# A seventh and a fourth pair by seven products in the two halves of the output projection, and a fixed order of the tail's passage to its seeded banks

## The chip, the cores and the metric

The kernel runs on one core of one Trainium2 chip. The metric is the device time of one execution in microseconds (us), of which smaller is better. Three runs of the kernel before gave 905.26 us in the median (904.65 to 905.49).

## The reference, cut to what matters

One layer of a hybrid decoder (DEPTH is 1, so the recurrence layer never runs), in float32, for one sequence of 256 tokens, width 2048 and branch width 4096:

```
h = rmsnorm(x, norm_g); h, gate = adaln(h, c, ada_w, ada_b)
b_gate, c_gate, v, g = split(h @ w_in, 4)              # 256 x 2048 by 2048 x 16384
y = b_gate * causal_conv(c_gate * v, conv_w) * silu(g) # 256 x 4096
x = x + gate * (y @ w_out)                             # 256 x 4096 by 4096 x 2048
return rmsnorm(x, final_g)
```

The change touches the last product, `y @ w_out`, and what leads from it to the output.

## The kernel before, in words

**Split products.** Every float32 operand of a matmul is split into a high part (a cast on ScalarE, `split_hi`, L352) and a low part (a subtraction on VectorE, `split_lo`, L357), and a product is three matmuls: high by high, high by low, low by high (`triple`, L722). Each weight tile of 128 x 2048 elements (1 MB) is loaded by SyncE's queue (`load_o`, L711), cast by ScalarE, subtracted by VectorE, and used by TensorE.

**Rings.** Weight tiles live in three rings of three buffers: `lo` holds the raw weights of the output projection and the sums made of them, `hi` the high parts, `raw` the low parts. A load can be issued only when the last reader of the buffer's former content is through, which is nearly always a VectorE subtraction; a cast and a subtraction wait in the same way for TensorE to be through with the buffers that they overwrite.

**The output projection.** The 4096 rows of `w_out` are 32 blocks of 128, taken in 16 pairs; `y` of a pair is one tile of 128 x 2 x 2 x 256 (two blocks, high and low, 256 tokens). `columns` (L771) takes 1024 output columns at a time and walks the pairs in an order written by hand. A plain pair costs one split and 24 matmuls of 512 columns (2 token tiles, 2 blocks, 2 column halves, 3 each). A pair in `sevens` goes by a Strassen form instead (`seven`, L736): seven products, 21 matmuls, of four sums of the weights (L742, L744, L745 on VectorE) and four sums of `y` (`token_forms`, L632), with two casts and two subtractions (L743 and L746 for the weights, L352 and L357 for their sums). The sums of `y` of the pairs in `SEVEN` are made while the projection in runs, where each pair's `y` arises. Three products go to separate banks (`p1`, `p6`, and `p75` with two) that `gather` (L761) adds up on VectorE and ScalarE behind the last such pair, through a 128 x 512 scratch `u2` at the end of the tile `big`.

- First 1024 columns: the pairs in the order 0, 1, 10, 2, 11, 3, 12, 4, 13, 5, 14, 6, 15, 7, 8, 9, those from 10 on by seven. Behind it VectorE adds the banks to the gathered sums (L809) and `gated` (L726) multiplies by the gate and adds the residual, in the time of the second 1024 columns.
- Second 1024 columns: 0, 1, 2, 10, 3, 13, 11, 4, 14, 12, 5, 15, with 10, 11, 12 by seven. Pairs 6 to 9 (`LAST`) come after it: first for column half 2 (`halves[0]`, both token tiles), then for column half 3, whose weights are multiplied by the gate first (L862). For half 3, what is there so far is gated, added to the residual and written back by ScalarE into two banks `po[0]` and `po[1]`, one for each token tile (L847 to L850: the seeded banks); the last 48 matmuls add to them, the first 24 to `po[0]`, the last 24 to `po[1]`.
- `finish(t)` (L815) squares `po[t]` on ScalarE with its sum (L877), takes the root (L818, with a change of ScalarE's function table before the first), the reciprocal (L819), and scales and stores four pieces of 128 x 512 (L820 to L829).

**What sets the order.** The order on each engine is that of a scheduler which lays the traced instructions out by its own times; `later`, `behind` and `in_order` (L165 to L194) bend it by hand. Each engine runs its list in order.

**Token tiles.** The normalised tokens lie in `hT` (14 of the 16 blocks of 128) and `hT2` (the last two); the buffers are used again, that of `hT` for `big` (residual, `final_g`, `u2`), that of `hT2` for the sums of `y` of pair 15.

Of the kernel before, what the change touches and what calls it, by code (L numbers as in the profile page):

```python
# [8 lines left out]
F32 = mybir.dt.float32  # L9
# [108 lines left out]
def short_conv_layer(ctx: ExitStack, tc: tile.TileContext, x, c, norm_g, ada_w, ada_b, w_in, conv_w, w_out, final_g, out):  # L118
# [175 lines left out]
    KB = KT - 2  # L294
    hT = hpool.tile([P, KB, 2 * T], F32R, tag="big", name="hT")
    hT2 = hpool.tile([P, KT - KB, 2 * T], F32R, tag="big2", name="hT2")

    def tokens(k, part):
        return (hT[:, k] if k < KB else hT2[:, k - KB])[:, part * T : (part + 1) * T]
# [329 lines left out]
    SEVEN = range(10, 16)  # L629
    forms = {}  # L630

    def token_forms(pair, u):  # L632

        sums = zs[0][:, 1].rearrange("p a (b f) -> p (a b) f", f=P)
        a11, a12 = u[:, 0, 0:P], u[:, 1, 0:P]
        a21, a22 = u[:, 0, P:T], u[:, 1, P:T]
        s1n, s2, s3, s4 = (sums[:, j] for j in range(4))
        nc.vector.scalar_tensor_tensor(out=s1n, in0=a21, scalar=-1.0, in1=a22, op0=ALU.mult, op1=ALU.subtract)
# [3 lines left out]
        if pair < 14:  # L642
            form = adap.tile([P, ASLOT], F32R, tag="at", name="form", bufs=4).rearrange("p (h s f) -> p h s f", h=2, f=P)
            hi, lo = form[:, 0], form[:, 1]
        elif pair == 14:
            hi, lo = (adap.tile([P, 512], F32R, tag="gv", name="form_g").rearrange("p (s f) -> p s f", f=P) for _ in range(2))
        else:
            form = hpool.tile([P, 2, 4, P], F32R, tag="big2", name="form_h")
            hi, lo = form[:, 0], form[:, 1]
        forms[pair] = hi, lo  # L650
        nc.scalar.copy(hi, sums)
        nc.vector.tensor_tensor(out=lo, in0=sums, in1=hi.bitcast(F32), op=ALU.subtract)

    for ct in range(NS, NCT, 2):
        for q in QUARTERS:
# [28 lines left out]
            else:  # L684
                nc.vector.tensor_tensor(out=u, in0=bank, in1=u, op=ALU.mult)
                split_y(ys[ct // 2], u)
                if ct // 2 in SEVEN:
                    token_forms(ct // 2, u)
# [5 lines left out]
    big = hpool.tile([P, 3 * D + W], F32, tag="big", name="big")  # L694
    xr = big[:, 0 : TT * D].rearrange("p (t f) -> p t f", t=TT)
    fg = big[:, TT * D : 3 * D]
    u2 = big[:, 3 * D :]
# [100 lines left out]
    def wide_bank(name):  # L798
# [5 lines left out]
        0, (0, 1, 10, 2, 11, 3, 12, 4, 13, 5, 14, 6, 15, 7, 8, 9), SEVEN,  # L804
# [10 lines left out]
    def finish(t):  # L815
# [20 lines left out]
        2 * W, (0, 1, 2, 10, 3, 13, 11, 4, 14, 12, 5, 15), SEVEN[0:3],  # L836
# [8 lines left out]
    for t in range(TT):  # L845
        c = ends[t][:, 1]
        nc.vector.tensor_tensor(out=c, in0=halves[1][:, t], in1=c, op=ALU.add)  # L847
        nc.vector.tensor_tensor(out=c, in0=c, in1=gate(3), op=ALU.mult)
        nc.vector.tensor_tensor(out=c, in0=c, in1=xr[:, t, 3 * W : 4 * W], op=ALU.add)
        nc.scalar.copy(po[t], c)  # L850
# [6 lines left out]
    late = []  # L857
    for ep in LAST:
# [4 lines left out]
        hi, lo = split(raw, SLOT, "raw")  # L863
# [39 lines left out]
```

## Time and profile before

| | |
|---|---|
| runs | 905.26 us median, 904.65 to 905.49 |
| profiled execution, its own time | 905.34 us |
| its span in the trace | 903.6 us |
| PE busy, DVE busy, ACT busy | 888.2, 670.2, 482.4 us |
| mean granted clock of PE | 0.998 |

The page gives for each engine its busy time, for each line of the kernel the number and mean length of its instructions and what the engine had waited for, and the chain of work that ended last. PE is TensorE, PEld its weight loads, DVE VectorE, ACT ScalarE, SPq the DMA queue of SyncE. In a timeline a row is one instruction or a run of equal ones: start, length, engine, line, operation, output and inputs, count, and in brackets the idle time of the engine just before it with what ended it.

### The profile page before, as it was taken

The numbers are of one execution on the slowest core, as the hardware profiler recorded it, in microseconds if no ns is written. First come the engines' busy times: TensorE is split into PE (matmuls) and PEld (weight loads), VectorE is DVE, ScalarE is ACT, GpSimd is POOL, SyncE is SP. The second block draws the span as 40 slices with busy tenths as digits, with TensorE's granted clock in tenths as the row PEclk, the third lists the DMA queues.
The fourth block names the chain that finished last, engine by engine and source line by source line (L and its number), as shares of the span: only waits on it lengthen the run. The fifth ranks groups of instructions, "written<-read, shape, count | busy, mean of one in ns | idle before, by whom it ended". The sixth has DMA issues, their size and how long they took to land.

```text
span 903.6 us, 16403 instructions
## 1 busy us (share of the span) xinstructions
PE 888.2 (98%) x7000; PEld 851.0 (94%) x7000; DVE 670.2 (74%) x661; ACT 482.4 (53%) x427; POOL 87.3 (10%) x95
## 2 busy tenths in 40 slices
PE   7999999999999999999999999999999999999996
PEld 4899999999999999999999999999999988888884
DVE  5889989888888867765875677565555578889685
ACT  6767866665548756644433434443434435544443
POOL 0000000000000132024324303320000000000000
PEclk9999999999999999999999999999999999999999
DMA  9999999999998587687988888866666486675652
GB/s 309 366 368 368 363 313 354 353 369 351 351 328 286 162 279 247 187 257 236 287 238 241 257 279 263 248 211 200 188 187 190 138 304 209 212 251 163 214 182 94
DMA packets 159594, 235.01 MB, mean 260 GB/s; under 512 B 6804, under 2 KB 105284, under 8 KB 159136
## 3 DMA queue, kind: packets, MB, share of 16 engines
q1 hardware_dynamic: 156384, 226.56, 76.7%
q0 software_dynamic: 3008, 7.34, 2.8%
q8 instruction: 55, 0.90, 0.4%
q14 instruction: 19, 0.16, 0.1%
q10 hardware_dynamic: 128, 0.04, 0.0%
HBM read 224.49 MB, written 2.10 MB: 251 GB/s over the span
## 4 chain that ended last, share of the span: by engine, by line
PE 90%; DMA 4%; DVE 2%; ACT 1%; SPq 1%; issue 1%; ACTq 0%
PE mm_b L491 39%; PE mm_s L491 36%; PE mm_w L722 7%; PE mm_o L722 5%; PE mm L722 4%; DMA at<-in_ada_w_dram 2%; DVE lo L357 1%; SPq L231 1%; DMA raw_s<-in_sc_w_in_dram 1%; ACT hi L352 1%; DMA x<-in_x_dram 1%; DMA raw_o<-in_sc_w_out_dram 1%; PE tp_g L481 0%; DVE raw_o L862 0%; ACT mm_s L524 0%
## 5 line engine op out<-in xcount | busy, mean ns | idle before, releaser
L491 PE MATMUL mm_s<-hT,hi 128*128 128x256 f32 x2048 | 350.3, 277 | 1.8 <-ACT hT L328 1.0
L491 PE MATMUL mm_b<-hT,hi 128*128 128x256 f32 x2048 | 348.2, 276 | 0.0
L491 PEld LDWEIGHTS mm_s<-hT,hi 128*128 128x128 f32 x2048 | 308.1, 188 | 2.4 <-ACT hT L328 1.2
L491 PEld LDWEIGHTS mm_b<-hT,hi 128*128 128x128 f32 x2048 | 308.6, 188 | 0.0
L491 PE MATMUL mm_b<-hT,lo 128*128 128x256 f32 x1024 | 282.6, 276 | 0.0
L491 PE MATMUL mm_s<-hT,lo 128*128 128x256 f32 x1024 | 282.0, 277 | 0.1
L357 DVE TENSOR_TENSOR lo<-raw,hi 128x2048 fp32r<-128x2048 f32 (+1 forms) x66 | 151.8, 2301 | 101.4 <-ACT hi L352 101.1
L352 ACT CAST hi<-raw 128x2048 fp32r<-128x2048 f32 (+1 forms) x66 | 123.7, 1875 | 191.6 <-PE mm_b L491 150.7
L491 PEld LDWEIGHTS mm_b<-hT,lo 128*128 128x128 f32 x1024 | 192.2, 188 | 0.0
L491 PEld LDWEIGHTS mm_s<-hT,lo 128*128 128x128 f32 x1024 | 191.7, 188 | 0.3 <-DVE lo L357 0.3
L357 DVE TENSOR_TENSOR lo<-raw_s,hi 128x2048 fp32r<-128x2048 f32 (+1 forms) x80 | 149.3, 1872 | 39.6 <-ACT hi L352 39.1
L352 ACT CAST hi<-raw_s 128x2048 fp32r<-128x2048 f32 (+1 forms) x80 | 123.9, 1557 | 56.1 <-PE mm_s L491 51.7
L474 DVE SCALAR_TENSOR_TENSOR gv<-at,silu_c,gv 128x512 f32<-128x512 f32 x105 | 78.6, 749 | 3.6 <-DMA at<-in_ada_w_dram 1.9
L512 ACT COPY acc<-mm_s 128x1024 f32<-128x1024 f32 x54 | 54.7, 1013 | 42.4 <-PE mm_s L491 42.3
L357 DVE TENSOR_TENSOR lo<-raw_o,hi 128x2048 fp32r<-128x2048 f32 x23 | 52.5, 2289 | 25.7 <-ACT hi L352 25.7
L352 ACT CAST hi<-raw_o 128x2048 fp32r<-128x2048 f32 x23 | 43.8, 1908 | 48.4 <-PE mm_o L722 17.3
L722 PE MATMUL mm_o<-hi,y 128*128 128x512 f32 x188 | 59.0, 389 | 0.0
L722 PE MATMUL mm_w<-hi,y 128*128 128x512 f32 x184 | 58.8, 389 | 0.0
L623 POOL TENSOR_TENSOR gacc<-gacc,z 128x512 f32<-128x512 f32 x28 | 45.9, 1639 | 119.3 <-DMA z<-gacc 119.3
L617 DVE SCALAR_TENSOR_TENSOR gacc<-at_g,silu_c,gacc 128x512 f32<-128x512 f32 x60 | 45.9, 764 | 8.0 <-DMA at_g<-in_ada_w_dram 6.9
L621 POOL DMA_DIRECT2D z<-gacc x28 | 15.7, 561 | 330.6 <-DVE acc L558 284.9
L722 PEld LDWEIGHTS mm_o<-hi,y 128*128 128x128 f32 x188 | 35.3, 188 | 7.3
(152 smaller groups left out, 675.4 us busy)
## 6 DMA issues: line engine op xcount, KB each, us to landing
raw<-in_sc_w_in_dram SPq DMA_DIRECT2D x64, 1024.0 KB, 5.8
raw_s<-in_sc_w_in_dram SPq DMA_DIRECT2D x47, 1024.0 KB, 7.7
raw_o<-in_sc_w_out_dram SPq DMA_DIRECT2D x32, 1024.0 KB, 5.2
at<-in_ada_w_dram SPq DMA_DIRECT2D x114, 256.0 KB, 7.8
raw_s<-in_sc_w_in_dram SPq DMA_DIRECT2D x33, 512.0 KB, 6.7
at_g<-in_ada_w_dram SPq DMA_DIRECT2D x32, 512.0 KB, 7.8
at<-in_ada_w_dram SPq DMA_DIRECT2D x6, 512.0 KB, 9.3
x<-in_x_dram SPq DMA_DIRECT2D x4, 512.0 KB, 6.2
```

The costliest lines, as they stand in the source:

```text
L231: nc.sync.dma_start(at[:, :, s, :], adas[:, j : j + kk, s, 0 : NK0 * P])
L352: nc.scalar.copy(hi[:, :n], raw[:, :n])
L357: nc.vector.tensor_tensor(out=lo[:, :n], in0=raw[:, :n], in1=hi[:, :n].bitcast(F32), op=ALU.subtract)
L474: nc.vector.scalar_tensor_tensor(out=gv, in0=at4[:, i], scalar=c_k, in1=gv, op0=ALU.mult, op1=ALU.add)
L491: mm = last_mm[0] = nc.tensor.matmul(dst, w, h[k], start=begins and left, stop=ends, skip_group_check=True)
L512: nc.scalar.copy(acc[ch, q], bank)
L617: nc.vector.scalar_tensor_tensor(out=ga, in0=at3[:, i, :], scalar=s, in1=ga, op0=ALU.mult, op1=ALU.add)
L621: nc.gpsimd.dma_start(turned[0 : P - away], ga[away:P])
L623: nc.gpsimd.tensor_tensor(out=ga, in0=ga, in1=turned, op=ALU.add)
L722: nc.tensor.matmul(dst, y[a], b, start=opens and i == 0, stop=ends and i == 2, skip_group_check=True)
```

## The change

1. The token tiles are cut 12, 2, 2 (`hT`, `hT2`, `hT3`), and `big` loses `u2`, so that a second buffer of the size of `hT2` comes free for sums of `y`. `gather` uses a half of `ends[1]` as its scratch.
2. Pair 9 joins `SEVEN`. Its sums of `y` are made late: `late_form` adds the high and low part of `y` of pair 9 again and calls `token_forms`, in the first 1024 columns behind the load of the seventh pair of the order.
3. First 1024 columns: 0, 1, 10, 2, 11, 3, 12, 4, 13, 5, 14, 6, 15, 9, 7, 8, with seven pairs by seven (10 to 15 and 9).
4. Second 1024 columns: 0, 1, 2, 10, 3, 11, 4, 12, 5, 13, 14, 15, with four pairs by seven (10 to 13).
5. The passage to the seeded banks is split by token tile and put in a fixed order on each engine with the two gated weight tiles of half 3: gate the first weights, `move(0)`, split them, gate the second, cast them, `move(1)`, subtract. The matmuls into `po[0]` are traced behind both splits, those into `po[1]` still behind `finish(0)`; the scheduler orders them anew. What follows on half 2 is held behind that order.

```diff
-    KB = KT - 2
+    KB = KT - 4
     hT = hpool.tile([P, KB, 2 * T], F32R, tag="big", name="hT")
-    hT2 = hpool.tile([P, KT - KB, 2 * T], F32R, tag="big2", name="hT2")
+    hT2 = [hpool.tile([P, 2, 2 * T], F32R, tag=f"big{i}", name=f"hT{i}") for i in (2, 3)]
...
-    SEVEN = range(10, 16)
+    SEVEN = range(9, 16)
+    LAST_FORM = 9
...
-            form = hpool.tile([P, 2, 4, P], F32R, tag="big2", name="form_h")
+            form = hpool.tile([P, 2, 4, P], F32R, tag="big2" if pair == 15 else "big3", name="form_h")
...
-    big = hpool.tile([P, 3 * D + W], F32, tag="big", name="big")
+    big = hpool.tile([P, 3 * D], F32, tag="big", name="big")
...
-        add(u2, p6, ends[0][:, 1])
-        add(ends[1][:, 1], p75[:, 0], u2)
-        add(ends[0][:, 0], p75[:, 1], u2)
+        add(ends[1][:, 0], p6, ends[0][:, 1])
+        add(ends[1][:, 1], p75[:, 0], ends[1][:, 0])
+        add(ends[0][:, 0], p75[:, 1], ends[1][:, 0])
         add(ends[1][:, 0], p75[:, 1], ends[1][:, 1])
+
+    def late_form():
+        u = zs[1][:, 1]
+        y = ys[LAST_FORM]
+        nc.vector.tensor_tensor(out=u, in0=y[:, :, 0].bitcast(F32), in1=y[:, :, 1].bitcast(F32), op=ALU.add)
+        token_forms(LAST_FORM, u)
...
             if loads:
                 loads(n - 4)
+                if n == 6:
+                    late_form()
...
-        0, (0, 1, 10, 2, 11, 3, 12, 4, 13, 5, 14, 6, 15, 7, 8, 9), SEVEN,
+        0, (0, 1, 10, 2, 11, 3, 12, 4, 13, 5, 14, 6, 15, 9, 7, 8), (10, 11, 12, 13, 14, 15, 9),
...
-        2 * W, (0, 1, 2, 10, 3, 13, 11, 4, 14, 12, 5, 15), SEVEN[0:3],
+        2 * W, (0, 1, 2, 10, 3, 11, 4, 12, 5, 13, 14, 15), (10, 11, 12, 13),
...
+    def move(t):
+        c = ends[t][:, 1]
+        nc.vector.tensor_tensor(out=c, in0=halves[1][:, t], in1=c, op=ALU.add)
+        nc.vector.tensor_tensor(out=c, in0=c, in1=gate(3), op=ALU.mult)
+        nc.vector.tensor_tensor(out=c, in0=c, in1=xr[:, t, 3 * W : 4 * W], op=ALU.add)
+        nc.scalar.copy(po[t], c)
...
+    with in_order():
+        raw_a = gated_piece(LAST[0])
+        move(0)
+        late = [(LAST[0], *split(raw_a, SLOT, "raw"))]
+        raw_b = gated_piece(LAST[1])
+        hi_b = split_hi(raw_b, SLOT)
+        move(1)
+        late.append((LAST[1], *split_lo(raw_b, SLOT, hi_b, "raw")))
+    for ep, hi, lo in late:
         out_mm(po[0], 0, ep, hi, lo)
-        late.append((ep, hi, lo))
     for t in range(TT):
         c = ends[t][:, 0]
-        nc.vector.tensor_tensor(out=c, in0=halves[0][:, t], in1=c, op=ALU.add)
-        gated(t, 2 * W, W, c, c, 1)
+        with behind(ended):
+            nc.vector.tensor_tensor(out=c, in0=halves[0][:, t], in1=c, op=ALU.add)
+            gated(t, 2 * W, W, c, c, 1)
```

Up to the output projection every engine's list is as before. Three places of the lists matter for the prediction. The first is VectorE at the end of the first 1024 columns. Before, it stood so, from pair 15's weights and their sums (`raw_o_8725`, `sums_o_8727`) to the plain pair 7 (`raw_o_8765`):

```order
L742 TENSOR_TENSOR sums_o_8727<-raw_o_8725 128x1024
L744 TENSOR_TENSOR sums_o_8727<-raw_o_8725,sums_o_8727 128x512
L745 TENSOR_TENSOR sums_o_8727<-raw_o_8725,sums_o_8727 128x512
L746 TENSOR_TENSOR lo_8729<-raw_o_8725,hi_8728 128x1536
L357 TENSOR_TENSOR lo_8737<-sums_o_8727,hi_8735 128x2048
L357 TENSOR_TENSOR lo_8769<-raw_o_8765,hi_8767 128x2048
```

In the changed kernel pair 15 (`raw_o_8734`, `sums_o_8736`) is followed by pair 9 by seven (`raw_o_8769`, `sums_o_8771`) and then by pair 7 (`raw_o_8809`):

```order
L746 TENSOR_TENSOR lo_8738<-raw_o_8734,hi_8737 128x1536
L742 TENSOR_TENSOR sums_o_8771<-raw_o_8769 128x1024
L357 TENSOR_TENSOR lo_8746<-sums_o_8736,hi_8744 128x2048
L744 TENSOR_TENSOR sums_o_8771<-raw_o_8769,sums_o_8771 128x512
L745 TENSOR_TENSOR sums_o_8771<-raw_o_8769,sums_o_8771 128x512
L746 TENSOR_TENSOR lo_8773<-raw_o_8769,hi_8772 128x1536
L357 TENSOR_TENSOR lo_8781<-sums_o_8771,hi_8779 128x2048
L357 TENSOR_TENSOR lo_8813<-raw_o_8809,hi_8811 128x2048
```

Two pairs by seven now follow each other without a plain one between them, and the first sum of pair 9's weights stands ahead of the last subtraction of pair 15. In these rings the buffer of `raw_o_8769` is that of pair 6's weights, and the buffer of `raw_o_8809` is that of `sums_o_8736`.

The second place is VectorE in the second 1024 columns, ahead of the plain pair 4 (`raw_o_9074`), in the changed kernel; pair 11 is `raw_o_9039`, pair 12 `raw_o_9104`:

```order
L357 TENSOR_TENSOR lo_9013<-raw_o_9009,hi_9011 128x2048
L744 TENSOR_TENSOR sums_o_9041<-raw_o_9039,sums_o_9041 128x512
L745 TENSOR_TENSOR sums_o_9041<-raw_o_9039,sums_o_9041 128x512
L746 TENSOR_TENSOR lo_9043<-raw_o_9039,hi_9042 128x1536
L357 TENSOR_TENSOR lo_9051<-sums_o_9041,hi_9049 128x2048
L742 TENSOR_TENSOR sums_o_9106<-raw_o_9104 128x1024
L357 TENSOR_TENSOR lo_9078<-raw_o_9074,hi_9076 128x2048
```

Before, two plain pairs (3 and 13, then 4 and 14) stood between the pairs by seven, and each sum came behind them; now there is one, and the first sum of pair 12 stands ahead of pair 4's subtraction.

The third place is the end of TensorE's list. Before, the last matmuls into `po[0]` (`mm_1_8868`) and the first into `po[1]` (`mm_1_8869`), 24 matmuls from the end:

```order
L722 MATMUL mm_1_8868<-hi_9340,y9_4461 128x512 x2
L722 MATMUL mm_1_8868<-lo_9342,y9_4461 128x512
L722 MATMUL mm_1_8868<-hi_9340,y9_4461 128x512
L722 MATMUL mm_1_8869<-hi_9321,y6_4444 128x512
L722 MATMUL mm_1_8869<-lo_9323,y6_4444 128x512
```

In the changed kernel, from the last matmuls into `po[0]` (`mm_1_8882`) to the last of all:

```order
L722 MATMUL mm_1_8882<-lo_9349,y9_4462 128x512
L722 MATMUL mm_1_8882<-hi_9343,y9_4462 128x512
L722 MATMUL mm_1_8883<-lo_9349,y8_4461 128x512
L722 MATMUL mm_1_8883<-hi_9343,y8_4461 128x512 x2
L722 MATMUL mm_1_8883<-lo_9349,y8_4461 128x512
L722 MATMUL mm_1_8883<-hi_9343,y8_4461 128x512
L722 MATMUL mm_1_8883<-hi_9343,y9_4462 128x512
L722 MATMUL mm_1_8883<-lo_9349,y9_4462 128x512
L722 MATMUL mm_1_8883<-hi_9343,y9_4462 128x512 x2
L722 MATMUL mm_1_8883<-lo_9349,y9_4462 128x512
L722 MATMUL mm_1_8883<-hi_9343,y9_4462 128x512
```

`po[0]` is now complete 11 matmuls before the end instead of 24: 13 of `po[1]`'s matmuls, those with the first weights of half 3, stand ahead of `po[0]`'s last 11.

More of the change, by code (lines that the diff above doesn't have):

```diff
@@ L290, in short_conv_layer @@
     nc.vector.reciprocal(rstd, rstd)
[L294 removed]
+    KB = KT - 4
     hT = hpool.tile([P, KB, 2 * T], F32R, tag="big", name="hT")
[L296 removed]
+    hT2 = [hpool.tile([P, 2, 2 * T], F32R, tag=f"big{i}", name=f"hT{i}") for i in (2, 3)]
     def tokens(k, part):
[L299 removed]
+        return (hT[:, k] if k < KB else hT2[(k - KB) // 2][:, k % 2])[:, part * T : (part + 1) * T]
     hh_ = [tokens(k, 0) for k in range(KT)]
@@ L641, in token_forms @@
         nc.vector.tensor_tensor(out=s4, in0=a12, in1=s2, op=ALU.subtract)
-        if pair < 14:
+        if 9 < pair < 14:
             form = adap.tile([P, ASLOT], F32R, tag="at", name="form", bufs=4).rearrange("p (h s f) -> p h s f", h=2, f=P)
@@ L686, in short_conv_layer @@
                 split_y(ys[ct // 2], u)
-                if ct // 2 in SEVEN:
+                if ct // 2 in SEVEN and ct // 2 != LAST_FORM:
                     token_forms(ct // 2, u)
@@ L843, in out_mm @@
             triple(bank, y_parts(ep * EP + i, t), hi[:, o], lo[:, o], False, ep == LAST[-1] and i == EP - 1)
[L845 to L850, printed above, removed]
     for ep in LAST:
@@ L856, in short_conv_layer, with gated_piece @@
             out_mm(halves[0][:, t], t, ep, hi, lo)
-    late = []
-    for ep in LAST:
+    def move(t):
[4 more added lines that the diff above has]
+        nc.scalar.copy(po[t], c)
+    def gated_piece(ep):
         raw = w_tile("lo", "raw_o")
```

5 lines of the change are left out of this document (2 added, 3 removed).

## The prediction

> **What bounds the kernel now.** I read the shares, the chain that ended last, and what PE waited for in the output projection (engine, line, what it waited for, us in total, times, longest).
>
> ```profile
> PE 888.2 (98%) x7000; PEld 851.0 (94%) x7000; DVE 670.2 (74%) x661; ACT 482.4 (53%) x427; POOL 87.3 (10%) x95
> ...
> PE 90%; DMA 4%; DVE 2%; ACT 1%; SPq 1%; issue 1%; ACTq 0%
> ...
> PE mm L722 <- ACT mm L850: 0.8, 1, 0.8
> ```
>
> PE sets the time: a matmul that goes is worth its whole length, as long as its operands still come in time, and a wait of PE is paid in full. In the whole output projection PE waits once, for the seeded bank.
>
> Next the timeline of one period of the first 1024 columns, a plain pair (6) and one by seven (15): DVE and ACT, two weight loads, and PE at both ends.
>
> ```profile
> 780.61 2.29 DVE L357 TENSOR_TENSOR lo<-raw_o,hi 128x2048 fp32r<-128x2048 f32 x1 [0.97 <-ACT hi L352]
> 782.82 1.22 DVE L742 TENSOR_TENSOR sums_o<-raw_o 128x1024 f32<-128x1024 f32 x1
> 784.07 0.69 DVE L744 TENSOR_TENSOR sums_o<-raw_o,sums_o 128x512 f32<-128x512 f32 x1
> 784.80 0.69 DVE L745 TENSOR_TENSOR sums_o<-raw_o,sums_o 128x512 f32<-128x512 f32 x1
> 785.41 1.75 DVE L746 TENSOR_TENSOR lo<-raw_o,hi 128x1536 fp32r<-128x1536 f32 x1
> 787.54 2.29 DVE L357 TENSOR_TENSOR lo<-sums_o,hi 128x2048 fp32r<-128x2048 f32 x1 [0.38 <-ACT hi L352]
> 790.81 2.29 DVE L357 TENSOR_TENSOR lo<-raw_o,hi 128x2048 fp32r<-128x2048 f32 x1 [0.97 <-ACT hi L352]
> ...
> 788.87 1.91 ACT L352 CAST hi<-raw_o 128x2048 fp32r<-128x2048 f32 x1 [1.35 <-PE mm_w L722]
> ...
> 795.16 1.91 ACT L352 CAST hi<-raw_o 128x2048 fp32r<-128x2048 f32 x1 [0.86 <-DMA raw_o<-in_sc_w_out_dram]
> ...
> 789.86 0.37 SPq L711 DMA_DIRECT2D raw_o<-in_sc_w_out_dram  x1
> ...
> DMA to landing us min/median/max: 5.0/5.2/5.7
> ...
> 788.62 0.39 PE L722 MATMUL mm<-hi,y 128*128 128x512 f32 x1
> ...
> 798.65 0.84 PE L722 MATMUL mm_w<-hi,y 128*128 128x512 f32 x3
> ```
>
> PE begins pair 15 at 788.62 and the 45th matmul behind at 798.65: 10.03 us over 44, 0.228 us each. A period is 790.81 - 780.61 = 10.20 us; DVE idles 0.97 + 0.38 = 1.35 of it, so its slack against PE is small. The load that is issued at 789.86, when the subtraction before it (787.54 + 2.29) frees its buffer, ends an ACT wait at 795.16, 5.3 us later; the median of nine loads there is 5.2.
>
> Last the tail, with PE's one wait.
>
> ```profile
> 874.45 2.29 DVE L862 TENSOR_TENSOR raw_o<-raw_o,gate 128x2048 f32<-128x2048 f32 x1
> ...
> 881.26 2.28 DVE L357 TENSOR_TENSOR lo<-raw_o,hi 128x2048 fp32r<-128x2048 f32 x1
> ...
> 883.65 0.39 PE L722 MATMUL mm_o<-hi,y 128*128 128x512 f32 x1
> 884.18 1.19 ACT L850 COPY mm<-z 128x512 f32<-128x512 f32 x2 [3.59 <-DVE z L849]
> ...
> 884.82 0.50 PE L722 MATMUL mm<-hi,y 128*128 128x512 f32 x1 [0.79 <-ACT mm L850]
> ...
> 887.26 0.39 PE L722 MATMUL mm<-lo,y 128*128 128x512 f32 x1
> ...
> 890.69 0.60 ACT L877 ACTIVATE z<-mm 128x512 f32<-128x512 f32 x1 [1.57 <-PE mm L722]
> ...
> 891.40 1.28 ACT L818 ACT_TABLE_LOAD   x1
> ...
> 893.22 1.34 ACT L828 ACTIVATE big<-big,fs 128x512 f32<-128x512 f32 x2 [0.23 <-DVE fs L819]
> ...
> 895.65 0.39 PE L722 MATMUL mm<-hi,y 128*128 128x512 f32 x1
> 896.07 0.60 ACT L877 ACTIVATE z<-mm 128x512 f32<-128x512 f32 x1 [1.51 <-PE mm L722]
> ```
>
> ACT squares token tile 0 at 890.69, changes its table, and ends that tile's scaling at 893.22 + 1.34 = 894.56, 3.87 us behind; it then idles 1.51 us until PE ends. Tile 0's finish lies wholly under PE's last 24 matmuls.
>
> **The change part by part.** The sum is made against the profiled execution, 905.34 us (span 903.6), 0.08 above the median of 905.26.
>
> *Matmuls removed.* One more pair by seven in each half, 24 to 21 matmuls: 6 x 0.228 = **-1.37**.
>
> *PE's wait in the tail.* The matmul behind 883.65 would start at 883.88 and starts at 884.82: 0.94. From 884.82 to 887.26 PE starts 10 more in 2.44 us instead of 2.28: 0.16. In the new order DVE moves tile 0 directly behind the first gating and only then subtracts; ahead of the first bank's copy stand two subtractions and a gating less than before (the rows at 874.45 and 881.26 and one more such, some 6.9 us), so the bank is seeded several us ahead of PE. What could be late next is the second weights' low part, DVE's last row of that passage: it is wanted only 26 matmuls, 5.9 us, behind the first of half 3. So **-1.10**.
>
> *Pair 9 behind pair 15.* By the order above DVE meets pair 9's first sum (L742) ahead of pair 15's last subtraction. Pair 9's weights go into pair 6's buffer, free at 780.61 + 2.29 = 782.90, so they land at about 788.13 (issue 0.03, 5.2). In the profiled period that subtraction ran at 787.54; now it stands behind the sum. DVE: sum 788.15 to 789.29 (rows without dependence start 0.08 before the end of the one ahead), subtraction to 791.58. Only then is the buffer of pair 15's sums free for pair 7's weights: they land at 796.81, ACT casts 1.91 to 798.72, DVE subtracts 2.29 to 801.04. PE, with pair 15 from 788.62, is through both pairs and two matmuls of pair 7 after 44, at 798.65. It has to wait for that low part: 801.08 - 798.65 = **+2.43**. Pair 15's own low part, which stands behind the waiting sum, is wanted after 14 matmuls (791.8) and there at 791.58. DVE's own work between (two subtractions and sums of pair 9, done about 796.9) is not what ends last, but parts of the wait show earlier, at pair 9's low parts. Each 0.1 us of a load's time counts twice in it; loads of 5.0 and 5.4 give 2.0 and 2.8. Against that wait, the plain pairs 8 and 0 that follow have room again.
>
> *The second 1024 columns.* DVE's gating of the first half lies there before as after:
>
> ```profile
> 810.93 1.22 DVE L809 TENSOR_TENSOR z<-mm_w,z 128x1024 f32<-128x1024 f32 x1
> 812.06 1.22 DVE L730 TENSOR_TENSOR z<-z,gate 128x1024 f32<-128x1024 f32 x1
> ...
> 820.01 1.75 DVE L746 TENSOR_TENSOR lo<-raw_o,hi 128x1536 fp32r<-128x1536 f32 x1
> ```
>
> Let T be the moment at which the first half's last matmul is through. From L809's second row to the end of pair 10's L746 it is 10.83 us here, plus 1.13 for pair 10's first sum, which now stands behind it: T + 12.0. That frees the buffer for pair 11's weights: T + 17.2. Then DVE's rows in order: sum 1.14, pair 3's subtraction 2.21, two sums 0.72 and 0.61, L746 1.75: T + 23.7, and pair 12's weights land at T + 28.9. Pair 12's first sum stands ahead of pair 4's subtraction: 1.14 + 2.29, T + 32.4. PE needs that low part after 141 matmuls from T - 0.2 (four plain pairs, two by seven, three starts), T + 31.8: **+0.6**; with loads of 5.0 and 5.4, 0.2 and 1.0. Before, two plain pairs stood there and PE waited for nothing.
>
> *The end.* `po[0]` is complete 11 matmuls before the last: 11 x 0.228 = 2.51 us. ACT needs 3.87 from the first square to the end of tile 0's scaling, and its list has tile 1's square behind that. So tile 1's square waits 3.87 - 2.51 = **+1.36** behind PE's end, and everything behind it too. The table change of 1.28 us, hidden before, is on this path. [...]
>
> *Restarts.* After its wait PE lost 0.16 over ten matmuls in the tail; whether a restart costs that, the trace shows once only. Two restarts count (the earlier ones are inside the first wait): between 0 and 0.32, I take the row: **+0.3**.
>
> *Costed at nothing.* Pair 9's late sums of `y`:
>
> ```profile
> 723.31 2.29 DVE L357 TENSOR_TENSOR lo<-raw_o,hi 128x2048 fp32r<-128x2048 f32 x1 [2.50 <-ACT hi L352]
> ...
> 728.67 0.28 DVE L638 SCALAR_TENSOR_TENSOR z<-z 128x128 f32<-128x128 f32 x1
> ...
> 737.87 1.90 ACT L352 CAST hi<-raw_o 128x2048 fp32r<-128x2048 f32 x1 [3.02 <-issue]
> ...
> 739.80 2.29 DVE L357 TENSOR_TENSOR lo<-raw_o,hi 128x2048 fp32r<-128x2048 f32 x1 [2.54 <-ACT hi L352]
> ```
>
> The re-addition (0.69, as L744) falls into DVE's idle 2.50 us, four sums of 0.28 into the 2.54, the cast into ACT's 3.02; the subtraction of 0.69 behind pair 2's delays pair 11 by 0.6, of which the next period's idle 1.35 takes up all. Uncovered, these would cost 0.69 + 4 x 0.28 + 0.69 = 2.5 us of DVE. SyncE's queue now has the first residual load ahead of pair 2's weights; these are first touched at 737.87, some 11 us later, so a load's time more costs nothing. The scratch in `ends[1]` and the cut of the token tiles change no instruction's length.
>
> Sum: -1.37 - 1.10 + 2.43 + 0.6 + 1.36 + 0.3 = +2.2, so **907.6 us**. The measurement can tell about 0.2% (1.8 us) from no change; this is 0.25%.
>
> **Rivals.**
> *Waits shorter, the end as worked out.* If loads land faster when nothing else is under way, or lists overlap a little better, the waits of PE shrink; at 5.0 us and without restart costs the sum is 906.5, with the second half's wait and half of the first gone too 905.3. For it: a load of 5.0 is the minimum seen. Against: median 5.2. This ends within 0.2%.
> *Faster.* DVE's lead at pair 15 covers both pairs, that is, pair 9's weights land before DVE wants them. Then PE does not wait in either half, and the time is 905.34 - 1.37 - 1.10 = 902.9, with the end's 1.36 still paid 904.2. It decides at the load's issue: with 2.4 us less from pair 6's subtraction to the sum the wait is gone. Against: that buffer's reader ends at 782.90 and no load took under 5.0. Below 903.5 the end would have to be hidden as well, that is, ACT's chain would have to fit under 2.51 us.
> *Crowded loads.* The widest of nine took 5.7; twice per chain this adds 1 in each half: 909.6.
> *The clock.* PE's waits before pair 7 add to some 2.4 us within 10. The row of the stretch with PE's one wait (stretch, length, busy time and instructions of PE, PEld, DVE, ACT, POOL, granted clock, DMA share, GB/s):
>
> ```profile
> 880.00:890.00 10.00, 9.21 (x41) 7.26 (x40) 9.81 (x18) 3.10 (x7) 0.00 (x0) 1.00 0.01 2
> ```
>
> The clock stays full through 0.8 us. If three times that halved it over the next 21 matmuls, they would take 4.8 us longer: 912.4. [...]
>
> **How the numbers follow.** Forecast with the loads' spread (906.8 to 908.5): 0.62. Shorter waits (905.3 to 906.5): 0.19. Faster (902.9 to 904.2): 0.09. Crowded loads: 0.08. The clock: 0.02. 0.2% above the median is 907.1, within the forecast's own range: of its 0.62 about 0.12 lies below it. Slower by over 0.2%: 0.50 + 0.08 + 0.02 = 0.60; same: 0.12 + 0.19 + 0.02 (904.2 of the faster case) = 0.33; faster: 0.07. The range of 8 in 10 takes in the shorter waits, from 905.4, and ends at 908.8; it leaves out the faster case and the last two.
>
> **What would show it.** Waits of PE for DVE at L357 and L746 at pairs 9 and 7, 2.4 in all, and one of 0.6 at pair 4 of the second half; DVE idle before pair 9's L742, until the load; no wait of PE for ACT at the seeded banks; ACT's two squares 3.9 us apart and the second more than 1 us behind PE's last matmul. The prediction is wrong if PE's waits stay below 1 us, or if the second square follows PE's end at once.

## The result and the profile after

| | before | after |
|---|---|---|
| runs, us | 905.38 median (904.65 to 906.16, six) | 910.50 median (908.71 to 912.79, six) |
| ratio | | 1.0057, 95% interval 1.0043 to 1.0071 |
| profiled execution, its own time | 905.34 | 910.82 |
| span in the trace | 903.6 | 909.0 |
| mean granted clock of PE | 0.998 | 0.997 |

The kernel is slower by 5.1 us, where 2.2 were forecast; the time lies outside the range. The page of the kernel after, with the busy times, the chain that ended last, and `q8`, the queue of instructions that runs below tie to PE:

```profile
PE 888.6 (98%) x6994; PEld 849.3 (93%) x6994; DVE 678.5 (75%) x675; ACT 486.2 (53%) x430; POOL 89.8 (10%) x95
...
q8 instruction: 55, 0.90, 0.4%
...
PE 84%; DMA 7%; DVE 4%; ACT 2%; SPq 1%; issue 1%; ACTq 0%; DVEq 0%
```

PE has six matmuls less, and its share of the chain falls from 90% to 84%: DMA and DVE have taken 5 points. The waits of PE from 700 us on (engine, line, releaser: us, times, longest):

```profile
PE mm_o L722 <- DVE lo L357: 1.4, 1, 1.4
PE mm L722 <- ACT hi L743: 1.0, 1, 1.0
PE mm_w L722 <- DVE lo L357: 0.9, 1, 0.9
PE mm L722 <- DVE lo L746: 0.7, 1, 0.7
```

The wait for the seeded bank is gone; four others have come, two in the first 1024 columns (`mm_w`, and `mm` of L746), two in the second. The timeline of the kernel after at these places and at the end (DVE, PE, ACT):

```profile
780.96 2.29 DVE L357 TENSOR_TENSOR lo<-raw_o,hi 128x2048 fp32r<-128x2048 f32 x1 [1.52 <-ACT hi L352]
...
788.42 1.23 DVE L742 TENSOR_TENSOR sums_o<-raw_o 128x1024 f32<-128x1024 f32 x1 [0.91 <-DMA raw_o<-in_sc_w_out_dram]
789.56 2.28 DVE L357 TENSOR_TENSOR lo<-sums_o,hi 128x2048 fp32r<-128x2048 f32 x1
...
798.90 2.29 DVE L357 TENSOR_TENSOR lo<-raw_o,hi 128x2048 fp32r<-128x2048 f32 x1 [1.39 <-ACT hi L352]
...
843.50 1.23 DVE L742 TENSOR_TENSOR sums_o<-raw_o 128x1024 f32<-128x1024 f32 x1 [4.10 <-DMA raw_o<-in_sc_w_out_dram]
844.64 2.29 DVE L357 TENSOR_TENSOR lo<-raw_o,hi 128x2048 fp32r<-128x2048 f32 x1
...
788.45 0.39 PE L722 MATMUL mm<-hi,y 128*128 128x512 f32 x1
...
801.25 0.50 PE L722 MATMUL mm_w<-lo,y 128*128 128x512 f32 x1 [0.86 <-DVE lo L357]
...
845.03 0.51 PE L722 MATMUL mm<-hi,y 128*128 128x512 f32 x1 [0.98 <-ACT hi L743]
846.98 0.50 PE L722 MATMUL mm_o<-lo,y 128*128 128x512 f32 x1 [1.45 <-DVE lo L357]
...
888.37 0.39 PE L722 MATMUL mm_o<-hi,y 128*128 128x512 f32 x1
888.59 0.39 PE L722 MATMUL mm<-hi,y 128*128 128x512 f32 x1
...
899.25 0.39 PE L722 MATMUL mm<-hi,y 128*128 128x512 f32 x1
...
897.24 0.60 ACT L897 ACTIVATE z<-mm 128x512 f32<-128x512 f32 x1 [0.50 <-PE mm L722]
...
897.95 1.28 ACT L826 ACT_TABLE_LOAD   x1
...
901.01 0.57 ACT L897 ACTIVATE z<-mm 128x512 f32<-128x512 f32 x1
```

First half: from pair 15's first matmul (788.45) the 45th would start 44 x 0.228 later, at 798.48; it starts at 801.25, 2.77 late. Second half: VectorE stands 4.10 us in front of pair 12's first sum, for a load, with pair 4's subtraction behind it (844.64), and PE waits for both. At the seeded banks (888.37 to 888.59) PE goes on without a gap. At the end the squares are 3.77 apart, and the second starts 1.76 behind PE's last start; before it was 0.42.

The chain that ended last, from 780 to 850 us (start, us, what), names the loads that are on it:

```profile
783.28 5.05 DMA raw_o<-in_sc_w_out_dram
...
791.87 5.02 DMA raw_o<-in_sc_w_out_dram
...
801.22 6.37 DMA raw_o<-in_sc_w_out_dram
...
824.97 5.24 DMA raw_o<-in_sc_w_out_dram
...
836.75 6.65 DMA raw_o<-in_sc_w_out_dram
```

Pair 9's and pair 7's loads took 5.0, a little less than forecast. That of pair 1 of the second half took 6.4 and that of pair 12 there 6.7; that of pair 4, issued 3.0 us ahead of it, 7.1. The DMA view of the kernel after in the stretch 835.20 to 835.60 (packets, MB, share of 16 engines) and the line of the loads between 833.7 and 837.0 show what they have in common:

```profile
q8 instruction: 1, 0.02, 28.8%
```

```profile
DMA to landing us min/median/max: 6.7/6.9/7.1
```

One packet of instructions took one of the 16 engines for 0.288 x 16 x 0.4 = 1.84 us while both loads were under way. Such a packet comes every 28 to 31 us: here at about 743.8, 773.6, 804.4, 835.5, 865.1 and 893.5. The loads issued around the first five, at 741.92, 772.52, 801.22, 833.75 with 836.75, and 863.53, took 6.2 to 7.1; of the loads issued after 745 the others took 5.0 to 5.4, but for two right behind a late one (5.9 and 5.6). PE's 6994 matmuls and as many weight loads are 254 instructions to each of the 55 packets on average.

What the spans add up to, with "lost" for what is left between PE's starts when 0.227 us for each matmul is taken off: six matmuls -1.37, the seeded bank -1.05, lost in the first half 2.81 (0.36 + 0.93 + 0.38 + 1.14), in the second 3.30 (0.33 + 1.14 + 1.83), the second square later by 1.34, from there to the span's end 0.55 longer (8.03 for 7.48; in the twelve profiles of this document it lies anywhere from 7.5 to 8.5), the projection's start 0.20 earlier: +5.4, against 5.5 measured (910.82 for 905.34).

### The profile page after: what moved, and what is told of

Its sections match the earlier page's. It is cut to its first block, busy times and chain, and to the rows that moved or that the text cites. A ratio compares the mean times of both kernels' runs of the same rounds, so it can differ in the third digit from the quotient of the medians.

```text
span 909.0 us, 16409 instructions
## 1 busy us (share of the span) xinstructions
PE 888.6 (98%) x6994; PEld 849.3 (93%) x6994; DVE 678.5 (75%) x675; ACT 486.2 (53%) x430; POOL 89.8 (10%) x95
## 4 chain that ended last, share of the span: by engine, by line
PE 84%; DMA 7%; DVE 4%; ACT 2%; SPq 1%; issue 1%; ACTq 0%; DVEq 0%
PE mm_b L491 38%; PE mm_s L491 36%; PE mm_o L722 4%; DMA raw_o<-in_sc_w_out_dram 4%; PE mm_w L722 4%; PE mm L722 2%; DVE lo L357 2%; DMA at<-in_ada_w_dram 2%; ACT hi L352 1%; DMA raw_s<-in_sc_w_in_dram 1%; SPq L231 1%; DMA x<-in_x_dram 1%; DVE lo L746 0%; PE tp_g L481 0%; DVE z L730 0%
## 5 line engine op out<-in xcount | busy, mean ns | idle before, releaser
L623 POOL TENSOR_TENSOR gacc<-gacc,z 128x512 f32<-128x512 f32 x28 | 52.2, 1866 | 123.1 <-DMA z<-gacc 123.1
L357 DVE TENSOR_TENSOR lo<-raw_o,hi 128x2048 fp32r<-128x2048 f32 x21 | 48.1, 2290 | 19.0 <-ACT hi L352 18.9
L352 ACT CAST hi<-raw_o 128x2048 fp32r<-128x2048 f32 x21 | 40.0, 1907 | 41.4 <-PE mm_o L722 10.7
L722 PE MATMUL mm_w<-hi,y 128*128 128x512 f32 x172 | 55.5, 389 | 0.0
L722 PE MATMUL mm_o<-hi,y 128*128 128x512 f32 x176 | 55.2, 389 | 0.0
L524 ACT COPY mm_s<-acc 128x1024 f32<-128x1024 f32 x38 | 38.6, 1016 | 2.7 <-DVE acc L514 1.9
```

Of the source, the lines that this page charges most:

```text
L352: nc.scalar.copy(hi[:, :n], raw[:, :n])
L357: nc.vector.tensor_tensor(out=lo[:, :n], in0=raw[:, :n], in1=hi[:, :n].bitcast(F32), op=ALU.subtract)
L524: nc.scalar.copy(bank, acc[ch, q])
L623: nc.gpsimd.tensor_tensor(out=ga, in0=ga, in1=turned, op=ALU.add)
L722: nc.tensor.matmul(dst, y[a], b, start=opens and i == 0, stop=ends and i == 2, skip_group_check=True)
```

## The experiments

My theory behind the result: three separate costs, the loads' chain in the first half, the same in the second with packets of instructions on top, and the end. Each run stands in this table with PE's loss in the two halves, in the same measure, and the start of the second square behind the start of PE's last matmul. The last three columns are read from one profiled execution of each run, the times from all of its executions.

| run | median us (range, runs) | ratio to before, 95% interval | first half | second half | second square |
|---|---|---|---|---|---|
| before | 905.38 | | 0 | 0 | 0.42 |
| after | 910.50 (908.71 to 912.79, 6) | 1.0057, 1.0043 to 1.0071 | 2.81 | 3.30 | 1.76 |
| first half put back | 907.13 (906.21 to 908.64, 9) | 1.0021, 1.0011 to 1.0031 | 0 | 1.71 | 1.76 |
| second half put back | 908.38 (907.73 to 909.21, 5) | 1.0036, 1.0022 to 1.0050 | 2.43 | 0 | 1.88 |
| first sums held | 907.36 (906.23 to 908.07, 10) | 1.0021, 1.0012 to 1.0030 | 1.78 | 0.10 | 2.15 |
| packets moved, start longer | 918.56 (918.00 to 918.96, 4) | 1.0146, 1.0132 to 1.0160 | 2.36 | 0.96 | 1.76 |
| packets moved a little | 909.16 (908.83 to 909.49, 5) | 1.0040, 1.0026 to 1.0053 | 2.46 | 1.47 | 1.78 |
| first half back, packets moved | 906.05 (905.50 to 908.34, 11) | 1.0009, 1.0001 to 1.0018 | 0 | 0.58 | 1.76 |
| passage alone | 905.72 (905.09 to 908.13, 11) | 1.0005, 0.9996 to 1.0014 | 0 | 0 | 1.83 |
| tail laid out anew | 908.58 (907.88 to 910.52, 5) | 1.0037, 1.0024 to 1.0049 | 2.50 | 2.09 | 0.42 |
| one plain pair between | 903.66 (903.03 to 907.67, 10) | 0.9982, 0.9973 to 0.9992 | 0.29 | 0 | 0.42 |
| two at the start | 903.46 (902.74 to 903.84, 11) | 0.9978, 0.9969 to 0.9987 | 0 | 0.27 | 0.43 |

### The halves apart

First half put back:

```diff
-                if n == 6:
+                if n == 6 and LAST_FORM in sevens:
...
-        0, (0, 1, 10, 2, 11, 3, 12, 4, 13, 5, 14, 6, 15, 9, 7, 8), (10, 11, 12, 13, 14, 15, 9),
+        0, (0, 1, 10, 2, 11, 3, 12, 4, 13, 5, 14, 6, 15, 7, 8, 9), range(10, 16),
```

> The first 1024 columns are put back (pairs 0, 1, 10, 2, 11, 3, 12, 4, 13, 5, 14, 6, 15, 7, 8, 9, six of them by seven, no late sums of y); the second 1024 columns and the tail stay as changed. Theory (two separate chains of loads, one in each half): PE's wait of 2.8 us around pairs 9 and 7 goes, 3 matmuls of 0.228 come back, and some 3 us of waiting at pair 12 and pair 4 of the second half stay: 910.5 - 2.8 + 0.7 = 908.4, between 907.6 and 909.3. Rival (the second half's wait is the first half's lateness handed on by VectorE): the second wait falls to the 0.6 that was forecast, and the time to 906.0.

Second half put back:

```diff
-        2 * W, (0, 1, 2, 10, 3, 11, 4, 12, 5, 13, 14, 15), (10, 11, 12, 13),
+        2 * W, (0, 1, 2, 10, 3, 13, 11, 4, 14, 12, 5, 15), (10, 11, 12),
```

> The second 1024 columns are put back (0, 1, 2, 10, 3, 13, 11, 4, 14, 12, 5, 15, three pairs by seven); the first 1024 columns and the tail stay as changed. Theory: the second half's wait of some 3 us goes and 3 matmuls come back, 910.5 - 3.0 + 0.7 = 908.2, between 907.4 and 909.2, with PE's wait around pairs 9 and 7 still there at 2.4 to 2.8. Rival (only the new order of the first half costs, and the second half's wait would come whatever stands there): PE still waits some 2 us or more in the second half and the time stays within 0.5 of 910.5 or above it.

PE's waits with the first half put back, and the time to landing of its loads of pairs 4 and 12 in the second half:

```profile
PE mm_o L722 <- DVE lo L357: 1.4, 1, 1.4
```

```profile
DMA to landing us min/median/max: 6.2/6.4/6.7
```

PE's waits with the second half put back:

```profile
PE mm_w L722 <- DVE lo L357: 1.1, 1, 1.1
PE mm L722 <- DVE lo L746: 0.5, 1, 0.5
```

Each half loses by itself, and with the old order neither does, as the theory had it. For the second run the size was right too (908.4 for 908.2). For the first, neither theory's was: of the second half's 3.30 us 1.71 stayed. So part of that wait was lateness out of the first half, and part was its own, here with a packet of instructions at 831.6 us in both loads.

### VectorE's order

```diff
+        with behind(through):
-        nc.vector.tensor_tensor(out=s[:, 0:2], in0=b[:, 1:3], in1=b[:, 0:1].to_broadcast([P, 2, W]), op=ALU.subtract)
+            nc.vector.tensor_tensor(out=s[:, 0:2], in0=b[:, 1:3], in1=b[:, 0:1].to_broadcast([P, 2, W]), op=ALU.subtract)
...
+    def low_done():
+        ins = nc.cur_bb.bb.instructions[-1]
+        through[ins.engine] = ins.name
```

`low_done` stands behind the last subtraction of every pair, so the first sum of the next pair by seven can't be put ahead of it.

> The changed kernel, but VectorE may take the first sum of a pair's weights only behind the last subtraction of the pair before it, so it never waits for a load ahead of a subtraction that is ready. Theory (the sum put ahead costs, since the subtraction behind it frees the buffer of the next load): the load of pair 7's weights is issued at about 790 us instead of 792, PE's wait around pairs 9 and 7 falls from 2.8 to about 1.0, and the wait at pair 4 of the second half from some 3 to 0.3: 910.5 - 1.8 - 2.7 = 906.0, between 905.2 and 907.5. Rival (two pairs by seven with none or one plain pair between them cost this whatever VectorE's order): PE's waits stay at 5 to 6 us in all and the time within 0.7 of 910.5.

VectorE's timeline in this run (L744 is the first sum):

```profile
788.04 2.29 DVE L357 TENSOR_TENSOR lo<-sums_o,hi 128x2048 fp32r<-128x2048 f32 x1 [0.38 <-ACT hi L352]
790.25 1.22 DVE L744 TENSOR_TENSOR sums_o<-raw_o 128x1024 f32<-128x1024 f32 x1
...
797.81 2.29 DVE L357 TENSOR_TENSOR lo<-raw_o,hi 128x2048 fp32r<-128x2048 f32 x1 [0.55 <-ACT hi L352]
```

and its waits of PE:

```profile
PE mm L723 <- DVE lo L748: 0.7, 1, 0.7
PE mm_w L723 <- ACT hi L352: 0.6, 1, 0.6
```

Pair 15's subtraction now comes first (788.04 for 789.56), pair 7's load is issued at 790.36 instead of 791.87, and pair 7's low part is ready 1.1 us earlier. The first half loses 1.78 instead of 2.81: the sum put ahead cost about 1.0 of it (0.6 by the runs at 2.4), less than the 1.8 expected. The rest is pair 9's own low part, which is late because two pairs by seven follow each other (0.92 with its restart), and the cast of its sums (0.86). In the second half the wait is gone; but the packet came at 836.6 there and both loads took 5.3 and less, so how much of that is the order and how much the packet, this run doesn't tell.

### The packets of instructions

The matmuls that fill PE's time at the start are cut into more, narrower ones, so that PE has more instructions ahead of everything else:

```diff
-    def idle(n):
+    def idle(n, parts):
         for _ in range(n):
-            nc.tensor.matmul(tp_idle, ident, ones[:, 0:1].to_broadcast([P, 512]), start=True, stop=True)
+            for i in range(parts):
+                a, b = i * 512 // parts, (i + 1) * 512 // parts
+                nc.tensor.matmul(tp_idle[:, a:b], ident, ones[:, 0:1].to_broadcast([P, b - a]), start=True, stop=True)
...
-    idle(IDLE[0])
+    idle(IDLE[0], 12)
...
-    idle(IDLE[1])
+    idle(IDLE[1], 4)
```

> The changed kernel, with the 8 matmuls that fill PE's time at the start cut into 56 of the same columns in sum, so that PE has 96 matmuls more ahead of everything else and nothing else changes. In the trace each packet of PE's instructions (0.02 MB, one about every 30 us, 1 to 2 us on one of the 16 DMA engines) falls into a load that lands late: those at 804 and 835 us into the loads of pairs 1, 4 and 12 of the second half, which took 6.4, 7.1 and 6.7 instead of 5.0 to 5.2. Theory (the packet delays the load, and that made the second half's wait larger than forecast): 96 matmuls of 0.227 move the packets 22 us forward, to about 782, 813 and 843 us, where no load or only the end of one is under way; the three loads take 5.0 to 5.3, the second half's wait falls from some 3 to 1.0 or less, and the time to 908.3, between 907.3 and 909.2. Rival (the two loads slow each other, being issued 3.0 us apart): the loads of pairs 4 and 12 still take 6.5 or more, and the time stays within 0.7 of 910.5.

The narrow matmuls took longer than I had thought: the projection began 10.2 us later (736.71 for 726.53), so the time itself, 8.1 us above the kernel after, answers to neither theory. Inside the projection the run is to be read from its own start. There the packets of the second half came 23.3 and 23.6 us earlier than in the kernel after, outside the three loads, and the loads of pairs 4 and 12, again 3.0 us apart, took:

```profile
DMA to landing us min/median/max: 5.1/5.2/5.3
```

PE lost 0.96 in the second half. To have this without the longer start, 12 matmuls more in the first group alone (`idle(IDLE[0], 3)`, `idle(IDLE[1], 1)`):

> The changed kernel, with the first 3 of the matmuls that fill PE's time at the start cut into 9 of a third of the columns each: 12 matmuls more in the trace (each runs twice), and PE's start as long as before. Cutting them into 40 columns and fewer had moved the packets of PE's instructions, but had also made the start 10.2 us longer; this one is to show the packets alone. They come 12 x 0.227 = 2.7 us earlier: at about 801.7, 832.5 and 862.3 us instead of 804.4, 835.2 and 865.0. Theory (a load lands late when a packet falls into it): the load of pair 1 of the second half is still hit and takes 6.2 to 6.4; those of pairs 4 and 12 are issued behind the packet and take 5.0 to 5.4 instead of 7.1 and 6.7; PE's wait in the second half falls from 3.3 to about 1.5, and the time to 908.7, between 907.8 and 909.6. Rival (the loads of pairs 4 and 12 are slow because they run side by side): they stay above 6.3 and the time within 0.6 of 910.5.

The packet of this run in the stretch 830.0 to 830.4, the loads of pairs 4 and 12 (issued at 833.32 and 836.32), and PE's waits:

```profile
q8 instruction: 1, 0.02, 20.2%
```

```profile
DMA to landing us min/median/max: 5.1/5.1/5.2
```

```profile
PE mm_o L724 <- DVE lo L359: 1.1, 1, 1.1
PE mm_w L724 <- DVE lo L359: 1.0, 1, 1.0
PE mm L724 <- DVE lo L748: 0.6, 1, 0.6
```

The packet came ahead of both loads, 5 us earlier than in the kernel after and not 2.7, and they took 5.1 and 5.2; the load of pair 1, still hit, took 6.5. The second half lost 1.47 instead of 3.30. The rival (loads side by side slow each other) falls: they run side by side here as there. The time is 909.16, forecast 908.7. The executions of this run (908.83 to 909.49) lie inside the range of the kernel after (908.71 to 912.79), so the times alone would not decide between the two; the loads and PE's waits do.

The same cut with the first half put back takes both additions away:

> The run with the first 1024 columns put back (six pairs by seven there, four in the second half), with PE's first fill-in matmuls cut in 9 as in the run that moved the packets a little. There PE waited 1.7 us at pair 4 of the second half, with a packet of instructions at 831.5 us in the loads of pairs 4 and 12 (6.7 and 6.2 us). The packet should now come 3 to 5 us earlier, ahead of both issues (830.5 and 833.5). Theory (of the second half's 3.3 us, one part is lateness from the first half, one the packet, and the rest the chain as forecast, 0.6): without the first two PE waits 0.1 to 0.8 there, the two loads take 5.0 to 5.4, and the time is 907.1 - 1.2 = 905.9, between 905.4 and 906.6. Rival (the chain itself was mis-sized: the order of the second half costs 1.5 or more also with loads of 5.2): the wait stays above 1.3 and the time within 0.5 of 907.1.

Its waits of PE, and the loads of pairs 4 and 12:

```profile
PE mm_o L724 <- DVE lo L359: 0.3, 1, 0.3
```

```profile
DMA to landing us min/median/max: 5.0/5.1/5.2
```

0.58 us are lost: the 0.6 that the prediction had worked out for this place. The moments agree as well. With T the end of the first half's last matmul, the prediction frees the buffers for the weights of pairs 11 and 12 at T + 12.0 and T + 23.7 and lets pair 12's land at T + 28.9; here these loads are issued at T + 11.9 and T + 23.7, and pair 12's lands at T + 28.7. In the kernel after the three are T + 13.0, T + 24.8 and T + 31.4.

### The end

> The kernel before with parts 1 and 5 of the change alone: pairs, orders and sums of y of both halves as before, the passage to the seeded banks and the end of TensorE's list as changed. Theory (by the terms of the forecast): PE's wait at the seeded bank goes, -1.10, tile 0's finish no longer hidden, +1.36: 905.4 + 0.26 = 905.6, between 905.2 and 906.2. Rival (the end costs less than it looks, the second square being late only because PE's list was cut short by the waits ahead): 904.3 to 904.8.

The edit is the first half's and the second half's diffs above, together. The two squares in that run, and PE's last matmul:

```profile
891.83 0.60 ACT L897 ACTIVATE z<-mm 128x512 f32<-128x512 f32 x1 [0.20 <-PE mm L722]
...
895.67 0.57 ACT L897 ACTIVATE z<-mm 128x512 f32<-128x512 f32 x1
...
893.84 0.39 PE L722 MATMUL mm<-hi,y 128*128 128x512 f32 x1
```

905.72 for 905.6: PE has no wait in the projection, and what the passage gains there, 1.1 us, it gives back at the end, where the second square starts 1.83 behind PE's last start instead of 0.42. This can't be told from no change. Next the changed kernel with the end alone laid out anew:

```diff
     with in_order():
         raw_a = gated_piece(LAST[0])
-        move(0)
-        late = [(LAST[0], *split(raw_a, SLOT, "raw"))]
+        hi_a = split_hi(raw_a, SLOT)
         raw_b = gated_piece(LAST[1])
         hi_b = split_hi(raw_b, SLOT)
+        move(0)
+        late = [(LAST[0], *split_lo(raw_a, SLOT, hi_a, "raw"))]
+        late.append((LAST[1], *split_lo(raw_b, SLOT, hi_b, "raw")))
         move(1)
-        late.append((LAST[1], *split_lo(raw_b, SLOT, hi_b, "raw")))
-    for ep, hi, lo in late:
-        out_mm(po[0], 0, ep, hi, lo)
+    with in_order():
+        for ep, hi, lo in late:
+            out_mm(po[0], 0, ep, hi, lo)
...
-            for ep, hi, lo in late:
-                out_mm(po[1], 1, ep, hi, lo)
+            with behind(ended):
+                for ep, hi, lo in late:
+                    out_mm(po[1], 1, ep, hi, lo)
```

> The changed kernel with another tail: the matmuls into po[1] are held behind the last into po[0], as they ran before the change, and both weight tiles of half 3 are gated and cast ahead of move(0), both subtracted ahead of move(1), so that the second low part is there when po[0] wants it. Theory (the end costs 1.36 because token tile 0's finish no longer fits under the matmuls left behind it): the square of tile 1 follows PE's last matmul by 0.2 to 0.3 us instead of 1.34, and the time is 910.5 - 1.2 = 909.3, between 908.6 and 910.0; the waits at pairs 9, 7, 4 stay. Rival (the second square is late for another reason, as the table change or the stores, so that tile 0 done earlier brings nothing): within 0.3 of 910.5, or above it if PE then waits for a low part or a bank in the tail.

Its squares and PE's last matmul:

```profile
892.80 0.60 ACT L900 ACTIVATE z<-mm 128x512 f32<-128x512 f32 x1
...
898.18 0.60 ACT L900 ACTIVATE z<-mm 128x512 f32<-128x512 f32 x1 [0.91 <-PE mm L722]
...
897.76 0.39 PE L722 MATMUL mm<-hi,y 128*128 128x512 f32 x1
```

The squares are 5.38 apart again, ACT waits 0.91 for PE ahead of the second, and it starts 0.42 behind PE's last start, 1.34 sooner. The time fell by 1.9 in the median, and by 2.9 from one profiled execution to the other. Of the 2.9, 1.34 are the end; the second half lost 2.09 instead of 3.30 in this profile (its loads of pairs 4 and 12 took 6.2 and 5.8) and the first 2.50 instead of 2.81, and there the edit changes nothing: up to 878 us PE, VectorE and ScalarE run the same lists in both.

### Laid out anew

The new tail, `through` as above, and in the first half a plain pair between pairs 15 and 9:

```diff
-        0, (0, 1, 10, 2, 11, 3, 12, 4, 13, 5, 14, 6, 15, 9, 7, 8), (10, 11, 12, 13, 14, 15, 9),
+        0, (0, 1, 10, 2, 11, 3, 12, 4, 13, 5, 14, 6, 15, 7, 9, 8), (10, 11, 12, 13, 14, 15, 9),
```

> The changed kernel with three things undone or mended, seven and four pairs by seven kept: the first half's order ends 15, 7, 9, 8, so that a plain pair stands between pairs 15 and 9; VectorE takes a pair's first sum of weights only behind the pair before it; and the tail of the run with both weight tiles gated first and po[0]'s matmuls ahead of po[1]'s. Theory (what the change lost is these waits and nothing else): no wait of PE above 0.5 us behind 726 us, 6 matmuls less, -1.37, and the bank's wait gone, -1.10: 905.4 - 2.4 = 902.9, between 902.3 and 904.2 if a packet of instructions falls into a load that matters. Rival (a seventh and a fourth pair are more than VectorE and the loads can feed, however they are laid out): the waits move to pair 9 or to the start of the second half, and the time is 905 or above.

The page of that run, and VectorE where pairs 7 and 9 are:

```profile
PE 887.4 (98%) x6994; PEld 849.8 (94%) x6994; DVE 682.5 (76%) x675; ACT 486.1 (54%) x430; POOL 87.6 (10%) x95
...
PE 94%; DMA 2%; ACT 2%; SPq 1%; issue 0%; DVE 0%; ACTq 0%
```

```profile
790.36 2.29 DVE L357 TENSOR_TENSOR lo<-raw_o,hi 128x2048 fp32r<-128x2048 f32 x1 [0.42 <-ACT hi L352]
792.57 1.23 DVE L744 TENSOR_TENSOR sums_o<-raw_o 128x1024 f32<-128x1024 f32 x1
```

The same matmuls, as many sums and as many loads as in the kernel after, in 6.8 us less; VectorE doesn't wait for a load at pair 9, and the view of PE's waits from 700 us on is empty. In this order `through` changes no engine's list, so that against the run with the tail alone (908.58) the one pair moved is worth 4.9 us. The kernel is 0.18% faster than before. Last, two pairs by seven in a row at another place:

```diff
-        0, (0, 1, 10, 2, 11, 3, 12, 4, 13, 5, 14, 6, 15, 7, 9, 8), (10, 11, 12, 13, 14, 15, 9),
+        0, (0, 1, 10, 11, 2, 12, 3, 13, 4, 14, 5, 15, 6, 9, 7, 8), (10, 11, 12, 13, 14, 15, 9),
```

> Seven and four pairs by seven, VectorE's first sums held behind the pair before, the tail as in the run with one plain pair between; but the first half's order is 0, 1, 10, 11, 2, 12, 3, 13, 4, 14, 5, 15, 6, 9, 7, 8: the two pairs by seven that follow each other without a plain one stand at the start, where VectorE idled 2.5 us ahead of each of two subtractions. Theory (two in a row cost PE only where VectorE has no lead of its own): no wait of PE above 0.5 us at pairs 10 and 11 or later, 903.6, between 902.8 and 904.4. Rival (two in a row cost some 2 us wherever they stand, since the load behind them waits for the second one's sums): PE waits 1.5 to 2.8 in all around 740 to 760 us, and the time is 905.2 to 906.2.

Its page:

```profile
PE 93%; DMA 3%; SPq 1%; ACT 1%; issue 0%; DVE 0%; ACTq 0%
```

No wait at pairs 10 and 11: two in a row cost nothing there. 903.46 is the lowest time of all; its interval overlaps with that of the run before it.

## Why the prediction was wrong, point by point

- *Matmuls removed, -1.37*: right (6994 for 7000, at 0.227 us from start to start).
- *PE's wait in the tail, -1.10*: right, measured 1.05; what could have been late next, the second low part, was not.
- *Pair 9 behind pair 15, +2.43*: right in mechanism and nearly in size. VectorE met pair 9's sum ahead of pair 15's subtraction, waited for its load (0.91), and pair 7's low part came last; 2.77 in the profiled run, 2.4 to 2.8 with its restarts in five profiles. The run with first sums held shows that the sum put ahead is 0.6 to 1.0 of it. The rest is the sequence of two where VectorE has no lead: with a plain pair between them the first half lost 0.29, with the two at a place where VectorE idles nothing.
- *The second 1024 columns, +0.6*: **this step failed, by its size: 3.30.** The chain was the right one, and with loads of 5.0 to 5.2 it costs 0.58, as the run without the first half's change and without the packet shows. I gave every load on it 5.0 to 5.4. Two things were left out. The loads of pairs 1, 4 and 12 took 6.4 to 7.1, because a packet of PE's instructions fell into them; moving the packets by 12 matmuls took 1.8 of the 3.30 away, and with the first half put back 1.1 of 1.71. And VectorE came late out of the first half: putting that half back took 1.6 away. That 1.6 isn't lateness alone, though, as four runs show. With the first half on time and no packet in the loads of pairs 4 and 12 the second half lost 0.58. With the first half as changed and no packet in any of the three loads (packets moved, start longer) the second half lost 0.96, with a packet in pair 1's load alone (packets moved a little) 1.47, with packets in all three 3.30. So lateness by itself adds 0.4 to the 0.58, the packet in pair 1's load 0.5, those in the loads of pairs 4 and 12 1.8, each step the difference of two profiled executions. The late load of pair 1 costs only a VectorE that is late already: in the run that lost 0.58 it took 6.1.
- *The end, +1.36*: right, 1.34 by the squares, and by the run that lays the tail out anew. What stands behind the second square took 0.55 longer; the profiles scatter by more than that there, and no run tells whether the change has a part in it.
- *Restarts, +0.3*: 0.1 us or so behind each of four waits, inside the losses above.
- *Costed at nothing*: right. PE waits nowhere between 726 and 790 us, so the late sums of `y`, the cast and the load put ahead of pair 2's weights are hidden.
- *Rivals*: "crowded loads" came nearest with 909.6, but not by what it said: loads 3.0 us apart took 5.0 to 5.3 where no packet fell. The granted clock was 1.00 in every stretch up to 903 us, through waits of up to 1.45 us; it was 0.50 only from 904 us on, behind PE's last matmul (899.25), which makes the mean 0.997. The trace of before has such late loads already: those of 742.12, 772.73, 800.27 and 856.42 took 5.7, 5.7, 6.3 and 6.7 with packets at 743.3, 773.7, 802.2 and 859.6; I took the widest that I had read, 5.7, for scatter.

## What to carry to other kernels

When a load comes onto the path that sets the end, price it by the slowest that the trace has (6.4 to 7.1 us here, against a median of 5.2) and ask what was under way beside it, rather than by the median of loads that nobody waited for. An operation that waits for a load should not stand ahead of one that frees the buffer of the next load (0.6 to 1.0 us here); two expensive stages in a row belong where the engine that feeds them has idle time, and here the place of one pair was worth 4.9 us, twice what the matmuls and the wait removed are. A last piece of work that hides under TensorE's tail needs its full length there: 3.87 us don't fit under 2.51.

## What the hardware showed that I had not expected

- A packet of PE's instructions (0.0164 MB; 254 matmuls and weight loads to a packet on average) occupies one DMA engine for 0.9 to 2.1 us, and a 1 MB load that was issued some 1 to 3 us ahead of it lands late: in the twelve profiles, behind 745 us, all 35 loads issued 0.9 to 3.2 us ahead of such a packet took 5.5 to 7.1 us (median 6.4), where loads with none near took 5.1 in the median. One issued 0.6 us ahead and one 4.3 us ahead took their usual time (5.1 in the run with first sums held, 5.2 in the kernel after), but one issued 4.4 us ahead took 6.6 (pair 1's with first sums held). Its place follows the number of PE's instructions: 96 matmuls more at the start moved the packets of the second half by 23.3 and 23.6 us. Where the loads in flight were on the path (pairs 4 and 12), moving the packet off them took 1.1 and 1.8 us from the second half's loss.
- The kernel after spread over 4.1 us in six runs, the one with its packets moved a little over 0.7 in five. That packets which fall at other moments from run to run make that spread is suggested by this, not shown.
- At the start, matmuls of 42 columns began 0.213 us apart (72 in 15.59 us), no closer than those of 128 columns behind them, where six of 512 took 5.26 in the kernel after: these narrow matmuls were not proportionally short. In both runs the distance of equal matmuls then halves, from 0.213 to 0.113 us for 128 columns at 24 us in the run with the narrow ones, from 0.853 to 0.433 for 512 columns between 9 and 10 us in the kernel after. What makes the halving, and why it comes 15 us later behind narrow matmuls, no run shows; the mean granted clock, 0.997 in both, doesn't tell.
